# Prompt attention with value products of two key blocks issued together

## The chip, the cores and the metric

The kernel runs on one core of a Trainium2 chip. The metric is device time in microseconds (us) of one execution; shorter is better. The core has a matrix engine (PE; PEld is its weight load), a vector engine (DVE), an activation engine (ACT), a general engine (POOL), which also issues the gathers by index, and SP, whose queue issues the other DMAs. Each engine runs its own instructions in a fixed order and waits for the others by semaphores.

## What is computed

One inference step of a one-layer decoder for a prompt of 1024 tokens and a sample group of 8 x 4 tokens, in float32. The stage that matters here is the attention of the prompt, for each block of 128 queries, with 8 heads in 2 groups:

```python
d_c = pos_q[:, None] - c_end[None, :]
s = jnp.einsum('bghtd,bgnd->bghtn', q, ck) * scale - slope * d_c
p_c = masked_probs(s, d_c >= 0)
o_c = jnp.einsum('bghtn,bgnd->bghtd', p_c, cv)            # compressed keys
...
o_s = jnp.einsum('bghtn,bgtnd->bghtd', p_s, vs)           # selected blocks
...
o_w = jnp.einsum('bghtl,bgld->bghtd', p_w, vw)            # window of 512
o = gate[0] * o_c + gate[1] * o_s + gate[2] * o_w
```

With 16 blocks of 64 keys in the prompt and the best 16 selected, the selected branch of the prompt is plain causal attention. The sample group does the same over 2048 cached tokens, of which it gathers the selected pages, and both groups also attend to 256 memory tokens.

## The kernel before, in words

The work is written as a Python program whose instructions a scheduler lays out once, ahead of time, into one order for each engine; it interleaves independent parts. Attention lies between the input projections and the output projection, at about 655 to 1067 us of the span. Three things run there side by side: the prompt's attention (`nsa_prompt`), the prompt's memory attention (`mem_unit`), and the sample group (`sample`).

The prompt's attention goes over 8 query blocks j, 2 head groups g and two branches b (causal and window); each (j, g, b) is a unit. A unit has three steps:

- **heads** (B): for each of 4 heads one or two tiles of scores S. Two matmuls (L837, L840) and masks (L839) make the scores, DVE takes the maximum (L845), ACT the exponential (L846) into a tile P. L840 needs QB, half of which POOL writes for each (j, g) in `prep` (L788).
- **fin**: the factors, and P times them (L878).
- **drain** (D): the unit's items are its key blocks of 128 and, in one branch, 63 compressed keys (cvp). For an item k, `tstep(k)` transposes P of the four heads on PE into one bank T (L891, two banks) and ACT copies T to PT in the buffer memory (L893, three buffers); `pvstep(k)` does two matmuls of 64 output columns each (L905), one for each half of the output partitions, that add V times PT to O (one bank). At the last item of both branches DVE multiplies O by the gates (L908) and SP stores it.

Drain steps wait in a queue of up to 14 and are woven between the heads of later units; in program order it is T0, T1, O0, T2, O1, T3, O2 and so on. There are 148 items in all.

The sample group works in two halves Q of four sequences, each in groups c = 4, 0, 1, 2, 3 of 512 keys. A group transposes its keys (L1495), multiplies them with the queries (L1502), and multiplies the probabilities with the values (L1527). Its rows lie in xs, seven buffers; for c = 0 to 3 POOL gathers them by index (L1336), four gathers in a group, and each waits until an earlier group's L1527 has freed its buffer. POOL runs in order, so a QB that stands behind gathers comes after them, and it waits for the landings of those ahead of it. New keys of the sample group are added by an extra product with VN (L1531), out of the probabilities P8 transposed (L1517).

Of the kernel before, what the change touches and what calls it, by code (L numbers as in the profile page):

```python
# [8 lines left out]
F32 = mybir.dt.float32  # L9
# [5 lines left out]
ALU = mybir.AluOpType  # L15
# [5 lines left out]
NP = 1024  # L21
# [80 lines left out]
class Build:  # L102
# [372 lines left out]
    def mem_unit(self, pool, psp, j):  # L475

        nc = self.nc
# [39 lines left out]
        PTs = []  # L517

        def tstep(k):
            def f():  # L520
                T = psp.tile([128, 512], F32, name="T", tag="T", bufs=2)
                for h in range(4):
                    o = h % 2 * 256 + k * 128
                    nc.tensor.transpose(T[:, h * 128:(h + 1) * 128], st["P"][h // 2][:, o:o + 128], self.ident)
                PT = pool.tile([128, 512], F32, name="PT", tag="PT", bufs=3)
                nc.scalar.activation(PT, T, AF.Copy)
                PTs.append(PT)
            return f
# [269 lines left out]
    def nsa_unit(self, pool, psp, j, g, b, ctx, prep, has_c):  # L798


        nc, mkb = self.nc, self.mkb
# [7 lines left out]
        for si, (a0, a1) in enumerate([(0, n0), (n0, nk)] if n0 < nk else [(0, nk)]):  # L809
            w = (a1 - a0) * 128  # L810
# [69 lines left out]
        items = []  # L880
# [3 lines left out]
        PTs = {}  # L884

        def tstep(k):
            def f():
                si, o, w, v = items[k]
                T = psp.tile([128, 512], F32, name="T", tag="T", bufs=2)
                for i in range(4):  # L890
                    nc.tensor.transpose(T[:w, i * 128:(i + 1) * 128], Ps[i, si][:, o:o + w], self.ident)  # L891
                PT = pool.tile([128, 512], F32, name="PT", tag="PT", bufs=3)
                nc.scalar.activation(PT[:w], T[:w], AF.Copy)  # L893
                PTs[k] = PT
            return f

        def pvstep(k):
            def f():
                _, _, w, v = items[k]
                if ctx["n"] == 0:  # L900
                    ctx["O"] = psp.tile([128, 512], F32, name="O", tag="O", bufs=1)
                O, n, total = ctx["O"], ctx["n"], ctx["total"]
                pv = PTs[k].rearrange("k (a c q) -> k c a q", a=2, c=2)
                for c in range(2):
                    nc.tensor.matmul(O[c * 64:(c + 1) * 64, :256], v, pv[:w, c], start=n == 0, stop=n == total - 1)  # L905
                ctx["n"] += 1
                if ctx["n"] == total:
                    nc.vector.tensor_tensor(ctx["gb"], O[:, :256], ctx["gb"], op=ALU.mult)  # L908
                    for a in range(2):
                        nc.sync.dma_start(self.s_mix[2 * g + a][:, j * 128:(j + 1) * 128], ctx["gb"][:, a * 128:(a + 1) * 128])  # L910
            return f

        def D():
            seq = [tstep(0)]
# [406 lines left out]
    def sample(self, pool, psp):  # L1321


        nc, A = self.nc, self.A
# [47 lines left out]
        for hd in range(8):  # L1372
            g, h = hd // 4, hd % 4
# [28 lines left out]
        BR = [32 * i for i in range(4)]  # L1402
# [2 lines left out]
        for b in range(8):  # L1405
            nc.sync.dma_start(run(A["new_win_s"][b, 0:508]), run(A["cache_win_kv"][b, 4:512]))

        VN = pool.tile([8, 2, 4, 128], F32, name="VN")
        nc.gpsimd.memset(VN, 0.0)
        for Q in range(2):  # L1410
            for i in range(2):
                nc.sync.dma_start(VN[i * 4:(i + 1) * 4, i], self.s_kv[1 + i][NP + Q * 16:NP + Q * 16 + 16, 128:256].rearrange("(b t) c -> t b c", t=4))

            ps = psp.tile([128, 512], F32, name="sS", tag="sS", bufs=2)
            for bb in range(4):
# [1 line left out]
            for bb in range(4):  # L1417
                b = Q * 4 + bb
# [55 lines left out]
            O = newO()  # L1474
# [6 lines left out]
            for c in (4, 0, 1, 2, 3):  # L1481
                xs = []
                for bb in range(4):
                    b = Q * 4 + bb
                    if c == 4:
                        x = load(A["cache_win_kv"][b].rearrange("(n l) f -> n l f", l=4))
                    else:
                        x = load(cslc, idx=idx4[:, c, b:b + 1])
                    xs.append(x)

                KT_ = []
                for a in range(4):
                    pt = pst()
                    for bb in range(4):
                        nc.tensor.transpose(pt[:, bb * 128:(bb + 1) * 128], xs[bb][:, a, 0:128], ident)  # L1495
                    KT_.append(pool.tile([128, 512], F32, name="KTs", tag="KTs", bufs=4))
                    evac(KT_[a], pt)
                S = psp.tile([128, 512], F32, name="sS", tag="sS", bufs=2)
                nc.tensor.matmul(S, sta[:, c], mov[:, int(c == 4)], start=True, stop=False, skip_group_check=True)
                for a in range(4):  # L1500
                    for bb in range(4):
                        nc.tensor.matmul(S[BR[bb]:BR[bb] + 32, a * 128:(a + 1) * 128], Qb[:, Q * 4 + bb], KT_[a][:, bb * 128:(bb + 1) * 128],  # L1502
                                         start=False, stop=True, skip_group_check=True)
                n_ = nm[:, c:c + 1]
                nc.vector.tensor_reduce(n_, S, axis=AX.X, op=ALU.max, negate=True)
                nw = {4: 1, 0: 0}.get(c)
                if nw is not None:
                    tt(n_, n_, nm[:, 5 + nw:6 + nw], op=ALU.min)
                    nc.scalar.activation(P8[:, nw * 4:nw * 4 + 4], SC[:, 128 + nw * 4:132 + nw * 4], AF.Exp, bias=n_, accum_out=s8[:, nw:nw + 1])
                P = pool.tile([128, 512], F32, name="sP", tag="sP", bufs=1)  # L1510
                nc.scalar.activation(P, S, AF.Exp, bias=n_, accum_out=sm[:, c:c + 1])
                if nw is not None:
                    tt(sm[:, c:c + 1], sm[:, c:c + 1], s8[:, nw:nw + 1], op=ALU.add)
                    pn = pst()
                    if nw:
                        nc.vector.memset(P8[:, 0:4], 0.0)
                    nc.tensor.transpose(pn[:8, 0:128], P8, ident)  # L1517
                    nc.vector.tensor_copy(PN, pn[:8, 0:128])
                pt = pst()
                for a in range(4):  # L1520
                    nc.tensor.transpose(pt[:, a * 128:(a + 1) * 128], P[:, a * 128:(a + 1) * 128], ident)
                PT = pool.tile([128, 512], F32, name="sPT", tag="sPT", bufs=2)
                evac(PT, pt)
                O = newO()
                for a in range(4):
                    for bb in range(4):
                        nc.tensor.matmul(O[BR[bb]:BR[bb] + 32, 0:128], PT[:, a * 128 + BR[bb]:a * 128 + BR[bb] + 32], xs[bb][:, a, 128:256],  # L1527
                                         start=a == 0, stop=a == 3 and nw is None)
                if nw is not None:
                    for bb in range(4):  # L1530
                        nc.tensor.matmul(O[BR[bb]:BR[bb] + 32, 0:128], PN[:, BR[bb]:BR[bb] + 32], VN[:, nw, bb], start=False, stop=True)  # L1531
                take(c, O)

            mn = pool.tile([128, 4], F32, name="mn", tag="mn", bufs=2)
# [306 lines left out]
```

## Time and profile before

| what | value |
|---|---|
| median of 3 runs | 2003.86 us (2001.06 to 2009.85) |
| profiled execution, device time | 2001.53 us |
| its span | 1999.8 us |
| mean granted clock of PE | 0.973 of full speed |
| PE busy | 1898.9 us, 95% of the span |
| DVE, ACT, POOL busy | 1154.1, 756.6, 434.3 us |
| attention, 655 to 1067 us of the span | 412 us: PE busy 386.84, DVE 306.05, ACT 282.69, POOL 62.40 |

A matmul's row in the trace runs from its start to a modelled end, and matmuls overlap, so what a group of matmuls costs is read from its start to the start of the next group, not from its length. Each L905 matmul leaves two records; an item's two matmuls stand as x4. "issue" is time in which an engine waited for nothing that the profile shows.

### The profile page before, as it was taken

The numbers are of one execution on the slowest core, as the hardware profiler recorded it, in microseconds if no ns is written. First come the engines' busy times: TensorE is split into PE (matmuls) and PEld (weight loads), VectorE is DVE, ScalarE is ACT, GpSimd is POOL, SyncE is SP. The second block draws the span as 40 slices with busy tenths as digits, with TensorE's granted clock in tenths as the row PEclk, the third lists the DMA queues.
The fourth block names the chain that finished last, engine by engine and source line by source line (L and its number), as shares of the span: only waits on it lengthen the run. The fifth ranks groups of instructions, "written<-read, shape, count | busy, mean of one in ns | idle before, by whom it ended". The sixth has DMA issues, their size and how long they took to land.

```text
span 1999.8 us, 33859 instructions
## 1 busy us (share of the span) xinstructions
PE 1898.9 (95%) x13280; PEld 1727.9 (86%) x13280; DVE 1154.1 (58%) x2759; ACT 756.6 (38%) x1696; POOL 434.3 (22%) x282
## 2 busy tenths in 40 slices
PE   8988999999996898999999999899999999999997
PEld 7987889999995666666657998799999999999997
DVE  6378897425535876786773216655455555544536
ACT  6301224226645576767673315122222111222222
POOL 2044331441102321022000213422121111121200
PEclk9989999999998799999999999899999999999999
DMA  7443333664336643333323322111111111111102
GB/s 267 149 132 92 101 86 96 189 184 168 114 117 133 196 138 105 125 99 103 105 86 114 87 76 88 32 53 53 43 43 53 43 43 43 43 43 53 43 1 87
DMA packets 197689, 191.31 MB, mean 96 GB/s; under 512 B 32925, under 2 KB 177046, under 8 KB 196314
## 3 DMA queue, kind: packets, MB, share of 16 engines
q1 hardware_dynamic: 190730, 153.86, 25.9%
q0 software_dynamic: 6800, 35.30, 5.3%
q8 instruction: 104, 1.70, 0.4%
q14 instruction: 55, 0.45, 0.1%
HBM read 155.34 MB, written 38.55 MB: 97 GB/s over the span
## 4 chain that ended last, share of the span: by engine, by line
PE 82%; DVE 7%; DMA 4%; issue 3%; ACT 2%; SPq 1%; POOL 1%; DVEq 0%; ACTq 0%; POOLq 0%
PE fps L122 12%; PE fps L124 12%; PE fps L123 12%; PE pso L122 4%; PE pso L124 4%; PE pso L123 4%; PE O L905 4%; PE T L891 4%; PE ops L122 2%; PE ops L124 2%; PE ops L123 2%; PE S L840 2%; PE S L837 2%; PE cps L630 1%; PE cps L122 1%
## 5 line engine op out<-in xcount | busy, mean ns | idle before, releaser
L1768 DVE TENSOR_TENSOR acc<-fps,acc 128x352 f32<-128x352 f32 (+3 forms) x360 | 185.3, 523 | 156.7 <-PE fps L124 156.7
L123 PE MATMUL fps<-h2lo,hi 128*128 128x352 f32 x768 | 248.1, 323 | 2.0 <-DVE h2lo L1712 2.0
L122 PE MATMUL fps<-h2hi,hi 128*128 128x352 f32 x768 | 247.7, 323 | 1.9 <-ACT h2hi L1711 1.9
L122 PE MATMUL fps<-yh,f2hi 128*128 128x352 f32 (+3 forms) x768 | 243.6, 326 | 6.0 <-DVE rm L1760 6.0
L123 PE MATMUL fps<-yl,f2hi 128*128 128x352 f32 (+3 forms) x768 | 247.1, 324 | 1.7 <-DVE yl L1745 1.7
L124 PE MATMUL fps<-h2hi,lo 128*128 128x352 f32 x768 | 248.7, 324 | 0.0
L124 PE MATMUL fps<-yh,f2lo 128*128 128x352 f32 (+3 forms) x768 | 246.6, 324 | 0.0
L1743 DVE TENSOR_TENSOR rl<-rl 128x352 f32<-128x352 f32 x96 | 132.0, 1376 | 145.3 <-ACT rl L1742 145.3
L118 POOL TENSOR_TENSOR lo<-raw,hi 128x1024 fp32r<-128x1024 f32 (+1 forms) x43 | 97.0, 2256 | 369.9 <-ACT hi L112 367.0
L118 POOL TENSOR_TENSOR f2lo<-raw,f2hi 128x1024 fp32r<-128x1024 f32 x32 | 79.6, 2487 | 363.1 <-ACT f2hi L112 354.9
L124 PE MATMUL pso<-hhi,wlo 128*128 128x352 f32 x480 | 157.3, 328 | 0.0
L123 PE MATMUL pso<-hlo,whi 128*128 128x352 f32 x480 | 157.2, 328 | 0.0
L122 PE MATMUL pso<-hhi,whi 128*128 128x352 f32 x480 | 157.2, 327 | 0.0
L122 PEld LDWEIGHTS fps<-yh,f2hi 128*128 128x128 f32 x768 | 144.7, 190 | 7.8 <-DVE rm L1760 6.3
L846 ACT ACTIVATE P<-S,nst 128x384 f32<-128x384 f32 (+4 forms) x264 | 127.3, 489 | 57.7 <-DVE nst L845 45.1
L123 PEld LDWEIGHTS fps<-yl,f2hi 128*128 128x128 f32 x768 | 145.5, 190 | 3.5 <-DVE yl L1745 2.0
L123 PEld LDWEIGHTS fps<-h2lo,hi 128*128 128x128 f32 x768 | 145.0, 189 | 2.3 <-DVE h2lo L1712 2.3
L122 PEld LDWEIGHTS fps<-h2hi,hi 128*128 128x128 f32 x768 | 144.9, 189 | 2.2 <-ACT h2hi L1711 2.2
L124 PEld LDWEIGHTS fps<-yh,f2lo 128*128 128x128 f32 x768 | 145.5, 190 | 1.4
L124 PEld LDWEIGHTS fps<-h2hi,lo 128*128 128x128 f32 x768 | 145.7, 190 | 0.0
L845 DVE TENSOR_REDUCE nst<-S 128x1 f32<-128x384 f32 (+4 forms) x264 | 109.8, 434 | 59.5 <-PE S L840 42.3
L112 ACT ACTIVATE f2hi<-raw 128x1024 fp32r<-128x1024 f32 x32 | 33.8, 1059 | 284.3 <-PE fps L123 269.1
(594 smaller groups left out, 4519.0 us busy)
## 6 DMA issues: line engine op xcount, KB each, us to landing
raw<-w_ff SPq DMA_DIRECT2D x64, 512.0 KB
wraw<-w_in SPq DMA_DIRECT2D x28, 512.0 KB
xs<-cache_mem_kv SPq DMA_DIRECT2D x16, 512.0 KB
s_gb<-st SPq DMA_DIRECT2D x36, 176.0 KB
x<-x_prompt SPq DMA_DIRECT2D x8, 512.0 KB
wraw<-w_mem_kv SPq DMA_DIRECT2D x8, 512.0 KB
qd<-s_q SPq DMA_DIRECT2D x32, 128.0 KB
ngb<-s_gb SPq DMA_DIRECT2D x64, 64.0 KB
```

Source lines behind the costliest of these rows:

```text
L118: eng.tensor_tensor(lo, src, hi.bitcast(F32), op=ALU.subtract)
L122: mm(ps, ahi, bhi, start=start, stop=False)
L123: mm(ps, ahi, blo, start=False, stop=False)
L124: mm(ps, alo, bhi, start=False, stop=stop)
L837: nc.tensor.matmul(S[:, :w], ctx["QA"][:, qs], KA[:, k0:k0 + w], start=True, stop=False)
L840: nc.tensor.matmul(S[:, :w], ctx["QB"][:, qs], KB[:, k0:k0 + w], start=False, stop=True)
L845: nc.vector.tensor_reduce(t[:, 0, pi, i:i + 1], S[:, o:o + pw], axis=AX.X, op=ALU.max, negate=True)
L846: nc.scalar.activation(P[:, o:o + pw], S[:, o:o + pw], AF.Exp, bias=t[:, 0, pi, i:i + 1], accum_out=t[:, 1, pi, i:i + 1])
L891: nc.tensor.transpose(T[:w, i * 128:(i + 1) * 128], Ps[i, si][:, o:o + w], self.ident)
L905: nc.tensor.matmul(O[c * 64:(c + 1) * 64, :256], v, pv[:w, c], start=n == 0, stop=n == total - 1)
L1743: tt(r, r, r, op=ALU.mult)
L1768: tt(acc[:, m, o:o + n], ps[:, :n], acc[:, m, o:o + n], op=ALU.add)
```

## The change

`pvstep` of an even item does nothing, unless it is the last; `pvstep` of an odd item k does the products of k and then of k - 1. So two items' products come one behind the other, after the transposes of the item that follows them. PT has four buffers in place of three, and for the room VN is halved: the two new-key parts lie in one tile, and P8's other half is zeroed each time (two more small memsets on DVE, one large one less on POOL).

```diff
-                PT = pool.tile([128, 512], F32, name="PT", tag="PT", bufs=3)
+                PT = pool.tile([128, 512], F32, name="PT", tag="PT", bufs=4)
...
         def pvstep(k):
             def f():
-                _, _, w, v = items[k]
-                if ctx["n"] == 0:
-                    ctx["O"] = psp.tile([128, 512], F32, name="O", tag="O", bufs=1)
-                O, n, total = ctx["O"], ctx["n"], ctx["total"]
-                pv = PTs[k].rearrange("k (a c q) -> k c a q", a=2, c=2)
-                for c in range(2):
-                    nc.tensor.matmul(O[c * 64:(c + 1) * 64, :256], v, pv[:w, c], start=n == 0, stop=n == total - 1)
-                ctx["n"] += 1
...
+
+                if k % 2 or k == len(items) - 1:
+                    pv1(k)
+                if k % 2:
+                    pv1(k - 1)
             return f
+
+        def pv1(k):
+            _, _, w, v = items[k]
+            if ctx["n"] == 0:
+                ctx["O"] = psp.tile([128, 512], F32, name="O", tag="O", bufs=1)
+            O, n, total = ctx["O"], ctx["n"], ctx["total"]
+            pv = PTs[k].rearrange("k (a c q) -> k c a q", a=2, c=2)
+            for c in range(2):
+                nc.tensor.matmul(O[c * 64:(c + 1) * 64, :256], v, pv[:w, c], start=n == 0, stop=n == total - 1)
+            ctx["n"] += 1
...
-        VN = pool.tile([8, 2, 4, 128], F32, name="VN")
-        nc.gpsimd.memset(VN, 0.0)
+        VN = pool.tile([8, 4, 128], F32, name="VN")
...
-                    if nw:
-                        nc.vector.memset(P8[:, 0:4], 0.0)
+                    nc.vector.memset(P8[:, 4 - nw * 4:8 - nw * 4], 0.0)
...
-                        nc.tensor.matmul(O[BR[bb]:BR[bb] + 32, 0:128], PN[:, BR[bb]:BR[bb] + 32], VN[:, nw, bb], start=False, stop=True)
+                        nc.tensor.matmul(O[BR[bb]:BR[bb] + 32, 0:128], PN[:, BR[bb]:BR[bb] + 32], VN[:, bb], start=False, stop=True)
```

The scheduler lays the whole of attention out anew. In the changed kernel L905 is L913, L1495 is L1501 and L1336 is L1343; L788, L837, L840 and L891 keep their numbers.

PE at the end of the last unit's drain, before (T are transposed blocks, O<-PT,V the products; the copy of T_n is PT_(n+5)):

```order
L905 MATMUL O_12789<-PT_12853,V1_6841 64x256 x2
L891 MATMUL T_12864<-ident_103,P_12630 128x128
L891 MATMUL T_12864<-ident_103,P_12663 128x128
L891 MATMUL T_12864<-ident_103,P_12698 128x128
L891 MATMUL T_12864<-ident_103,P_12731 128x128
L905 MATMUL O_12789<-PT_12860,V1_6841 64x256 x2
```

and after:

```order
L891 MATMUL T_12856<-ident_103,P_12631 128x128
L891 MATMUL T_12856<-ident_103,P_12662 128x128
L891 MATMUL T_12856<-ident_103,P_12697 128x128
L891 MATMUL T_12856<-ident_103,P_12732 128x128
L891 MATMUL T_12863<-ident_103,P_12631 128x128
L891 MATMUL T_12863<-ident_103,P_12662 128x128
L891 MATMUL T_12863<-ident_103,P_12697 128x128
L891 MATMUL T_12863<-ident_103,P_12732 128x128
L913 MATMUL O_12797<-PT_12861,V1_6841 64x256 x2
L913 MATMUL O_12797<-PT_12854,V1_6841 64x256 x2
```

Four transposes and one item's products in turn have become eight transposes and two items' products, the newer item's first.

POOL in the second half of the sample group, around the QBs of query block 6 (QB_11514 and 11741 before, QB_11515 and 11742 after; xs are gathered pages), before:

```order
L1336 DMA xs_8309<-cache_slc_kv,idx4_7260 128x1024 [waits PE_49]
L1336 DMA xs_8311<-cache_slc_kv,idx4_7260 128x1024 [waits DMASW7_49,PE_49]
L788 TENSOR_SCALAR QB_11514<-augq_6812,augj_6814 64x512 [waits DMASW3_49,DMASW2_49,DMASW4_49,DMASW1_49,DMASW5_49,DMASW0_49,DMASW6_49,DVE_49,PE_49]
L788 TENSOR_SCALAR QB_11741<-augq_6812,augj_6814 64x512 [waits DVE_49,PE_49]
L1336 DMA xs_8313<-cache_slc_kv,idx4_7260 128x1024 [waits PE_49,Pool_49]
L1336 DMA xs_8390<-cache_slc_kv,idx4_7260 128x1024 [waits PE_49]
L1336 DMA xs_8392<-cache_slc_kv,idx4_7260 128x1024 [waits PE_49]
L1336 DMA xs_8394<-cache_slc_kv,idx4_7260 128x1024 [waits PE_49]
```

and after:

```order
L1343 DMA xs_8310<-cache_slc_kv,idx4_7260 128x1024 [waits PE_49]
L1343 DMA xs_8312<-cache_slc_kv,idx4_7260 128x1024 [waits DMASW7_49,PE_49]
L1343 DMA xs_8314<-cache_slc_kv,idx4_7260 128x1024 [waits DMASW0_49,PE_49]
L1343 DMA xs_8391<-cache_slc_kv,idx4_7260 128x1024 [waits DMASW1_49,PE_49]
L1343 DMA xs_8393<-cache_slc_kv,idx4_7260 128x1024 [waits DMASW2_49,PE_49]
L1343 DMA xs_8395<-cache_slc_kv,idx4_7260 128x1024 [waits DMASW3_49,PE_49]
L788 TENSOR_SCALAR QB_11515<-augq_6812,augj_6814 64x512 [waits DMASW4_49,DMASW2_49,DMASW5_49,DMASW1_49,DMASW6_49,DMASW0_49,DMASW7_49,DVE_49,PE_49]
L788 TENSOR_SCALAR QB_11742<-augq_6812,augj_6814 64x512 [waits DVE_49,PE_49]
```

Both QBs now stand behind four more gathers, those that the sample product of group c = 1 sets free.

PE at the first use of that QB, before:

```order
L891 MATMUL T_11532<-ident_103,P_11264 128x128
L1521 MATMUL sS_8281<-ident_103,sP_8279 128x128 [waits Activation_49]
L1521 MATMUL sS_8281<-ident_103,sP_8279 128x128 x3
L837 MATMUL S_11558<-KA00_6816,QA_11513 128x448 [waits Activation_49]
L839 LDWEIGHTS idb_6810
L839 MATMUL S_11558<-mkb_6808,idb_6810 128x64
L840 MATMUL S_11558<-KB00_6820,QB_11514 128x448 [waits DVE_49,Pool_49]
```

and after:

```order
L1501 MATMUL sS_8337<-ident_103,xs_8308 128x128 [waits Activation_49]
L1501 MATMUL sS_8337<-ident_103,xs_8310 128x128
L1501 MATMUL sS_8337<-ident_103,xs_8312 128x128
L1501 MATMUL sS_8337<-ident_103,xs_8314 128x128
L840 MATMUL S_11559<-KB00_6820,QB_11515 128x448 [waits Pool_49]
L840 MATMUL S_11568<-KB00_6820,QB_11515 128x512
L837 MATMUL S_11575<-KA00_6816,QA_11514 128x448 [waits Activation_49]
```

The first use stood ahead of the product of group c = 1; it stands now behind that product and all 16 key transposes of group c = 2.

## Rows read from the trace of the kernel before

**Rows 1.** Page, part 1: busy time, share of the span, instructions.

```profile
PE 1898.9 (95%) x13280; PEld 1727.9 (86%) x13280; DVE 1154.1 (58%) x2759; ACT 756.6 (38%) x1696; POOL 434.3 (22%) x282
```

**Rows 2.** Busy time by stretch of attention: engines' us (instructions), PE clock, DMA share, GB/s.

```profile
740.00:780.00 40.00, 33.63 (x296) 23.72 (x296) 25.53 (x79) 22.86 (x68) 7.96 (x7) 0.91 0.44 131
...
860.00:900.00 40.00, 39.72 (x362) 27.07 (x360) 33.10 (x112) 27.73 (x87) 6.76 (x6) 1.00 0.40 118
...
1040.00:1067.00 27.00, 23.05 (x154) 12.81 (x154) 17.25 (x55) 18.55 (x48) 0.00 (x0) 1.00 0.21 64
```

**Rows 3.** Waits of PE in 655 to 1067 us: total us, times, longest.

```profile
PE S L840 <- POOL QB L788: 6.6, 2, 5.9
PE O L905 <- ACT PT L893: 6.1, 9, 1.6
```

**Rows 4.** Timeline at the end of the drain: start, us, engine, line, operation, xrecords.

```profile
1061.24 0.65 PE L905 MATMUL O<-PT,V 128*64 128x256 f32 x4
...
1061.82 0.66 PE L891 MATMUL T<-ident,P 128*128 128x128 f32 x4
...
1062.41 0.65 PE L905 MATMUL O<-PT,V 128*64 128x256 f32 x4
1062.58 0.60 ACT L893 ACTIVATE PT<-T 128x512 f32<-128x512 f32 x1 [0.57 <-PE T L891]
```

**Rows 5.** Timeline: transposes before scores, and two items' products in a row.

```profile
863.53 0.66 PE L891 MATMUL T<-ident,P 128*128 128x128 f32 x4
...
863.95 0.42 PE L837 MATMUL S<-KA,QA 128*128 128x384 f32 x1
...
867.24 1.08 PE L905 MATMUL O<-PT,V 128*64 128x256 f32 x8
...
868.25 0.44 PE L837 MATMUL S<-KA,QA 128*128 128x384 f32 x1
```

**Rows 6.** Timeline: sample product, scores before scores, scores before products, memory scores.

```profile
740.14 1.08 PE L1527 MATMUL sS<-xs,sPT 128*32 128x128 f32 x32
...
741.76 0.42 PE L840 MATMUL S<-KB,QB 128*128 128x384 f32 x1
...
742.02 0.34 PE L837 MATMUL S<-KA,QA 128*128 128x384 f32 x1
...
742.24 0.42 PE L840 MATMUL S<-KB,QB 128*128 128x384 f32 x1
...
742.58 0.65 PE L905 MATMUL O<-PT,V 128*64 128x256 f32 x4
...
745.36 0.28 PE L123 MATMUL S<-mklo,QA 128*128 128x256 f32 x1
...
745.48 0.28 PE L124 MATMUL S<-mkhi,QB 128*128 128x256 f32 x1
```

**Rows 7.** Timeline: one matmul of an item by itself (two records).

```profile
895.71 0.64 PE L905 MATMUL O<-PT,cvp 63*64 63x256 f32 x2
896.28 0.39 PE L1499 MATMUL sS<-smov,ssta 36*128 36x512 bf16 x1
```

**Rows 8.** POOL's timeline: gathers and QBs, with the idle time ahead and its releaser.

```profile
745.29 0.94 POOL L1336 DMA_INDIRECT xs<-cache_slc_kv,idx  x1 [0.30 <-PE S L840]
753.08 3.22 POOL L788 TENSOR_SCALAR QB<-augq,augj 64x512 fp32r<-64x512 bf16 x2 [6.85 <-issue]
...
922.89 3.22 POOL L788 TENSOR_SCALAR QB<-augq,augj 64x512 fp32r<-64x512 bf16 x2 [8.96 <-PE S L840]
931.05 1.18 POOL L1336 DMA_INDIRECT xs<-cache_slc_kv,idx  x1 [4.95 <-PE sS L1527]
...
935.06 0.95 POOL L1336 DMA_INDIRECT xs<-cache_slc_kv,idx  x1 [0.30 <-issue]
```

**Rows 9.** Gathers' line: DMA from issue to landing.

```profile
DMA to landing us min/median/max: 5.6/6.4/7.4
```

**Rows 10.** Stretch of 2 us behind the stall, columns as in Rows 2.

```profile
758.00:760.00 2.00, 2.00 (x10) 0.96 (x9) 1.48 (x6) 1.09 (x5) 0.00 (x0) 0.55 0.00 0
```

More of the change, by code (lines that the diff above doesn't have):

```diff
@@ L891, in f @@
                     nc.tensor.transpose(T[:w, i * 128:(i + 1) * 128], Ps[i, si][:, o:o + w], self.ident)
-                PT = pool.tile([128, 512], F32, name="PT", tag="PT", bufs=3)
+                PT = pool.tile([128, 512], F32, name="PT", tag="PT", bufs=4)
                 nc.scalar.activation(PT[:w], T[:w], AF.Copy)
@@ L898, in f @@
             def f():
-                _, _, w, v = items[k]
-                if ctx["n"] == 0:
-                    ctx["O"] = psp.tile([128, 512], F32, name="O", tag="O", bufs=1)
-                O, n, total = ctx["O"], ctx["n"], ctx["total"]
-                pv = PTs[k].rearrange("k (a c q) -> k c a q", a=2, c=2)
-                for c in range(2):
-                    nc.tensor.matmul(O[c * 64:(c + 1) * 64, :256], v, pv[:w, c], start=n == 0, stop=n == total - 1)
-                ctx["n"] += 1
[L907 to L910, printed above, removed]
-            return f
+                if k % 2 or k == len(items) - 1:
+                    pv1(k)
+                if k % 2:
+                    pv1(k - 1)
+            return f
+        def pv1(k):
[7 more added lines that the diff above has]
+            ctx["n"] += 1
+            if ctx["n"] == total:
+                nc.vector.tensor_tensor(ctx["gb"], O[:, :256], ctx["gb"], op=ALU.mult)
+                for a in range(2):
+                    nc.sync.dma_start(self.s_mix[2 * g + a][:, j * 128:(j + 1) * 128], ctx["gb"][:, a * 128:(a + 1) * 128])
         def D():
@@ L1406, in sample @@
             nc.sync.dma_start(run(A["new_win_s"][b, 0:508]), run(A["cache_win_kv"][b, 4:512]))
-        VN = pool.tile([8, 2, 4, 128], F32, name="VN")
-        nc.gpsimd.memset(VN, 0.0)
+        VN = pool.tile([8, 4, 128], F32, name="VN")
         for Q in range(2):
             for i in range(2):
-                nc.sync.dma_start(VN[i * 4:(i + 1) * 4, i], self.s_kv[1 + i][NP + Q * 16:NP + Q * 16 + 16, 128:256].rearrange("(b t) c -> t b c", t=4))
+                nc.sync.dma_start(VN[i * 4:(i + 1) * 4], self.s_kv[1 + i][NP + Q * 16:NP + Q * 16 + 16, 128:256].rearrange("(b t) c -> t b c", t=4))
             ps = psp.tile([128, 512], F32, name="sS", tag="sS", bufs=2)
```

## The prediction

> **What bounds the kernel now.** I read the page's busy times first: PE is busy 95% of the span and no other engine over 58% [rows 1]. Then the stretches of attention, since nothing outside it changes its work: in the stretch from 860 us PE is busy 39.72 of 40 us, while DVE has 33.10 and ACT 27.73; the stretch from 740 us has a hole (33.63 of 40, clock 0.91), and the last one, from 1040 us, another (23.05 of 27) with ACT at 18.55 [rows 2]. So PE time is worth its full length in most of attention, and little at its end. PE's waits name two of the holes: 6.6 us for QB, of which 5.9 in one wait, and 6.1 us in nine waits for a copy PT ahead of products [rows 3]. The reader is to see that PE's order has about 26 us of holes in 412 (412 less the 386.84 of the table), so a gain has to come out of PE's own instructions, and a new wait of a few us undoes much of it.
>
> **What a switch costs.** One item's products take 0.58 us to the start of the next transposes, and four transposes 0.59 us to the start of the next products [rows 4]. Two items in a row take 1.01 us to the scores behind them [rows 5], so the second item costs 0.43 and each run of products pays 0.15 us when PE leaves it. Four transposes ahead of scores take 0.42 [rows 5], so entering products from transposes costs 0.17. Scores of 384 columns take 0.26 us ahead of scores and 0.34 ahead of products [rows 6]: entering from scores costs 0.08.
>
> **The change, part by part.**
>
> *Fewer runs.* PE's order, counted: the 148 items stand in 141 runs of products before and in 83 after, 58 fewer. Leaving: 58 x 0.15 = 8.7 us. Entering from transposes (50 to 29): 21 x 0.17 = 3.6. From scores (58 to 37): 21 x 0.08 = 1.7. From the sample group's work (33 to 17), which no row prices: 16 between 0.08 and 0.17, 1.3 to 2.7; I take the middle, 2.0. Together 16.0 us less on PE, nearly all where PE is the bound.
>
> *Split items.* One of an item's two matmuls by itself takes 0.57 us [rows 7], as long as both together [rows 4]; torn apart, an item costs 0.43 more. The scheduler tears 3 items before and 5 after: 2 x 0.43 = 0.9 us lost.
>
> *Compressed keys in a run.* An item of 63 keys stands beside one of 128 in 3 places before and in 14 after. No row separates that switch from a wait for the copy. Bounds: 0, as inside a run, and 0.15, as on leaving one; 11 x 0 to 0.15 = 0 to 1.7 us. I take 0.8, the middle. The Trainium skill, page "TensorEngine Tiling (Array Packing)", section Key Properties, says that a change of the tiling mode, not of the tile alone, drains TensorE; whether 63 rows count as another mode it doesn't say. By it the loss is the upper end and the sum 0.9 us worse; no row here decides.
>
> *The wait for the newest copy.* After the transposes of k + 1 the products of k come first, whose copy is the newest but one, with one block of transposes between. Where only drain is left (five runs in the order), the two blocks of transposes take 0.42 + 0.59 = 1.01 us from the start of the first, while its copy ends 1062.58 + 0.60 - 1061.82 = 1.36 us after it [rows 4]: PE waits 0.35 us, a pair takes 1.01 + 0.35 + 1.01 = 2.37 instead of 2 x 1.17 = 2.34, and the gain there is gone. Elsewhere heads and sample work lie between: by the durations above the distance from a block's first transpose to its products is about 3.3 us in the middle of the list in both orders, and under 1.36 us in 3 items before and 10 after, 2.7 us short more than before. Today's waits for copies are 6.1 us though only three items are so near [rows 3], because ACT has other work ahead of the copy. I charge 3 us more; bounds 0 (the waits of today, halved in number, balance it) and 8 (they double, and the ten come on top).
>
> *The stall for QB at query block 3 stays.* POOL's QB there waits for gathers that a sample product sets free: the product starts at 740.14 [rows 6], the last of its four gathers is issued at 745.29, QB starts at 753.08, and two QBs take 3.22, so the first is there at 754.69, 14.6 us after the product [rows 8]. Nothing in that chain gets faster. PE has 2 runs fewer between (0.5 us) and one score head of 384 columns and its mask (0.56) moved behind it, so it comes 1.1 us earlier and waits 1.1 us longer than the 5.9 [rows 3]. 1.1 us lost.
>
> *A new stall for QB at query block 6.* Before, its QBs started at 922.89, released by PE, ahead of the gathers of 931.05 to 935.06 [rows 8]. In the new order four more gathers stand ahead of them, those that the product of group c = 1 frees, and POOL's QB waits for their landing. On PE there lie between that product's start and the first L840 that reads QB: 16 sample products (1.0 us), 16 key transposes and 16 transposes of P (32 x 0.105 = 3.4, a quarter of the 0.42 each), 4 items (4 x 0.43 = 1.7) in 3 runs (3 x 0.27 = 0.8 of switches), 12 memory score matmuls of 0.12 us, start to start (1.4) [rows 6], and five score matmuls with their masks at 0.26 (1.3): 9.6 us. The chain of the stall above took 14.6 us; with the shortest landing, 5.6 us [rows 9], it is 745.29 - 740.14 = 5.2 plus 5.6 plus 1.6 = 12.4. PE therefore waits 2.8 to 5.0 us; I take 5.0, the difference to the chain that the trace shows whole. The clock answers to such a wait: in the stretch from 758 us, behind the stall of 5.9 us, the granted clock is 0.55 [rows 10], so it was at the lower of its two levels (1.2 GHz) for 1.8 of the 2 us. If so ever since the stall's end at 754.7, that is 5.1 us of work that take 2.5 at 2.4 GHz. The new stall is a little shorter: I charge 2.0; bounds 0 and 2.5.
>
> *The rest.* A fourth PT takes a wait away from ACT only; no row shows ACT late for want of a buffer, so nothing. POOL loses a memset and DVE gains two small ones: neither engine is the bound [rows 2], nothing. The reads of VN come later than one half's did, which can delay a load of the second half of the sample group on SP; its reader is far behind, nothing.
>
> **Sum.** 16.0 - 0.9 - 0.8 - 3.0 - 1.1 - 5.0 - 2.0 = 3.2 us faster. Against the profiled execution, 2001.5 us of device time (span 1999.8), that is 1998.3. The median of the three runs lies 2.3 us above that execution, and the comparison will be with runs like them, so I set the forecast at 2003.9 - 3.2 = 2000.7 us. About 0.5%, 10 us, is what a measurement of this kernel can tell from no change.
>
> **The rivals.**
>
> *A, the new stall doesn't open.* If the gathers land faster at that place, or PE reaches the L840 late because it waited for keys and copies that would have cost it time anyway, 5.0 + 2.0 come back: gain 10.2, time 1993.7 us. For it: PE needs one of the same gathers for its key transposes ahead of the L840, so part of the wait is shared; landings vary from 5.6 to 7.4 us [rows 9]. Against: even the fastest chain is 2.8 us longer than PE's work.
>
> *B, slower: the newest copy rules.* ACT's copies come behind exponentials, and in each of the 58 merged places PE waits 0.35 us or more, as in the pure drain: 58 x 0.35 = 20 us in place of the 3. Then 3.2 + 3 - 20 = -14, time 2018 us. It turns the change into a loss from (3.2 + 3) / 0.35 = 18 places on. For it: the product wants the newer copy first. Against: the middle distance of 3.3 us is over twice the 1.36 us that a copy needs, and ACT has a quarter to a third of its time free where PE is bound [rows 2].
>
> *C, nothing comes through.* Other engines take PE's place as soon as it gets faster: DVE, at 33.10 of 40 us in the dense stretch [rows 2], has the least room. Gain 16.0 - 0.9 - 0.8 all gone into waits for scores, with the old stalls longer by as much: 2003.9 us. Against: DVE would be at 86% of the time if all 16 us came off attention.
>
> **How the numbers follow.** My forecast (stall and copies about as charged) 0.60 at 2000.7; A 0.22 at 1993.7; B 0.06 at 2018; C 0.12 at 2003.9. With every bound of my own case at its best end (0.7 more from entering, 0.8 from compressed keys, 3 from copies, 4.2 from the new stall) it would be 1992, at its worst (0.7, 0.9, 5 and 0.5) 2008. Faster by over 0.5% means below 1993.8: A's better half and the best end of my own case, 0.18. Slower by over 0.5%, above 2013.9: B, 0.06. Within 0.5%: 0.76. The range takes in all but B and the outer ends of A: 1991 to 2009.
>
> **What would show each step.** In the changed kernel's trace: two items' products in a row as x8 of about 1.01 us to the next start, some 58 times; PE's busy time in attention down by some 14 us while its waits are up by 8 to 10; one wait of PE at L840 for POOL QB of 6 to 8 us near 750 us and a second one of 3 to 6 us, not there before, near 890 to 900 us, with the clock at half behind both; waits of products for PT between 6 and 12 us, and 0.35 us in each pair at the end of the drain. The end of attention should come some 3 us earlier and all behind it be unchanged. I am wrong if the second stall isn't there (A), if products wait for PT by over 15 us (B), or if DVE is what PE's scores wait for (C).

## The result, and the profile after

The changed kernel takes 2016.95 us (median of 8 runs) where the kernel before takes 2002.45 (8 runs beside it): a ratio of 1.0072, 95% interval 1.0055 to 1.0089. It is 14.5 us slower; the forecast was 3.2 us faster, and the range ended at 2009.

Its profiled execution has a span of 2016.6 us. Nothing outside attention moved: attention starts 0.8 us earlier than before, and what follows attention takes 0.8 us longer, out of some 927. Attention grew. This is the page's row of busy times, against [rows 1]:

```profile
PE 1897.7 (94%) x13280; PEld 1740.2 (86%) x13280; DVE 1155.7 (57%) x2761; ACT 754.2 (37%) x1696; POOL 432.3 (21%) x281
```

PE is as busy as before although 58 runs of products fewer leave less to do; so part of its work ran slower. The stretches of attention (columns as in [rows 2]) show where, and the second fence has all of attention in the kernel before:

```profile
641.00:1089.00 448.00, 398.19 (x3309) 280.52 (x3309) 315.68 (x1025) 288.02 (x885) 63.38 (x50) 0.92 0.38 113
...
740.00:780.00 40.00, 30.46 (x277) 22.07 (x269) 23.99 (x74) 20.09 (x62) 8.08 (x7) 0.91 0.44 130
860.00:900.00 40.00, 38.67 (x337) 28.14 (x336) 31.72 (x103) 24.23 (x76) 8.10 (x8) 0.89 0.35 104
920.00:960.00 40.00, 34.04 (x316) 22.20 (x315) 22.12 (x66) 22.19 (x68) 7.03 (x7) 0.91 0.27 74
```

```profile
642.00:1073.00 431.00, 401.54 (x3309) 270.75 (x3308) 313.26 (x1023) 290.38 (x885) 63.97 (x50) 0.94 0.39 117
```

The same 3309 matmul records take 448 us instead of 431, with 50 us instead of 29 in which PE has nothing, and at a mean granted clock of 0.92 instead of 0.94. PE's waits in 655 to 1085 us (total us, times, longest), against [rows 3]:

```profile
PE S L840 <- POOL QB L788: 16.5, 3, 6.5
PE sS L1501 <- DMA xs<-cache_slc_kv,idx: 7.9, 3, 3.1
PE S L837 <- ACT P L846: 7.3, 3, 3.7
PE T L891 <- ACT PT L893: 4.9, 7, 1.4
PE O L913 <- ACT PT L893: 3.6, 10, 0.7
PE T L891 <- DVE P L878: 2.7, 2, 1.5
```

In the kernel before the first two were 6.6 [rows 3] and 1.8 us:

```profile
PE sS L1495 <- DMA xs<-cache_slc_kv,idx: 1.8, 4, 0.6
```

The waits for the copy PT have mostly moved from the products (6.1 us) to the transposes, which fill two T in a row and have only two.

This is the new stall at query block 6, from the timelines of PE and POOL:

```profile
927.23 1.08 PE L1532 MATMUL sS<-xs,sPT 128*32 128x128 f32 x32
...
932.32 0.95 POOL L1343 DMA_INDIRECT xs<-cache_slc_kv,idx  x1 [0.30 <-issue]
...
936.52 1.04 PE L1501 MATMUL sS<-ident,xs 128*128 128x128 f32 x8
...
941.66 3.22 POOL L788 TENSOR_SCALAR QB<-augq,augj 64x512 fp32r<-64x512 bf16 x2 [8.39 <-DVE P L515]
943.28 1.17 PE L840 MATMUL S<-KB,QB 128*128 128x448 f32 x2 [5.72 <-POOL QB L788]
```

The sample product at 927.23 frees the pages, the last of four gathers goes out at 932.32, QB starts 9.3 us later, and PE stands for 5.72 us. The gathers of this place (two of the four have a landing in the trace) took

```profile
DMA to landing us min/median/max: 7.9/8.4/8.9
```

so the last landed at 932.3 + 8.9 = 941.2 us, and QB starts 0.4 us later. The row names a DVE instruction that ended at about the same time; in a second profile of this kernel the last landing again lies 0.4 us ahead of QB and that DVE instruction ends 0.8 us before the landing, so the landing is what QB waits for. Behind the stall, and behind the wait for gathered pages that ends at 967.7, stretches of 2 us (the last three columns: granted clock, DMA share, GB/s):

```profile
943.00:945.00 2.00, 1.72 (x5) 1.19 (x5) 0.74 (x2) 0.41 (x2) 1.79 (x2) 0.50 0.00 0
945.00:947.00 2.00, 2.00 (x9) 0.77 (x8) 0.87 (x3) 0.00 (x0) 0.00 (x0) 0.50 0.04 8
947.00:949.00 2.00, 2.00 (x13) 0.91 (x11) 0.00 (x0) 0.00 (x0) 0.00 (x0) 0.98 0.00 0
...
967.00:969.00 2.00, 1.29 (x5) 1.09 (x6) 0.77 (x2) 0.57 (x2) 0.00 (x0) 0.64 0.91 301
969.00:971.00 2.00, 2.00 (x11) 1.60 (x10) 1.15 (x3) 1.58 (x7) 0.00 (x0) 0.51 0.21 56
```

After either wait PE works at 1.2 GHz (0.50) for 3 to 4 us before the grant returns to 2.4.

### The profile page after: what moved, and what is told of

It is laid out like the page before. It is cut to its first block, busy times and chain, and to the rows that moved or that the text cites. A ratio compares the mean times of both kernels' runs of the same rounds, so it can differ in the third digit from the quotient of the medians.

```text
span 2016.6 us, 33796 instructions
## 1 busy us (share of the span) xinstructions
PE 1897.7 (94%) x13280; PEld 1740.2 (86%) x13280; DVE 1155.7 (57%) x2761; ACT 754.2 (37%) x1696; POOL 432.3 (21%) x281
## 4 chain that ended last, share of the span: by engine, by line
PE 48%; DVE 2%; issue 1%; ACT 1%; DMA 1%; POOL 0%; DVEq 0%; SPq 0%; POOLq 0%; ACTq 0%
PE fps L122 12%; PE fps L124 12%; PE fps L123 12%; PE ops L122 2%; PE ops L124 2%; PE ops L123 2%; PE O L913 1%; PE T L891 1%; PE S L840 1%; DVE acc L1729 0%; PE S L837 0%; DMA mxr<-s_mix 0%; DMA xs<-cache_slc_kv,idx 0%; PE fps L1790 0%; DVE P L878 0%
```

## Attention taken apart

The same account was made for every kernel that was run. Length: from the matmul of L672 at attention's start to the first `ops` matmul that waited for the last copy. Waits: time in that stretch with no matmul record on PE. Lost at half clock: busy time at 1.2 GHz, from the granted clock of 1-us stretches, halved, since the same work would take half as long at 2.4 (an estimate). Rest: what is left, PE's work at full clock. Ratios are to the kernel before in the same comparison, with their 95% intervals.

| kernel (runs of products) | ratio | length | waits | lost at half clock | rest |
|---|---|---|---|---|---|
| before (141) | | 431.3 | 29.5 | 21.2 | 380.6 |
| unpaired_again, the same | 1.0001 (0.9975 to 1.0027) | 429.0 | 30.6 | 17.4 | 381.0 |
| changed (83) | 1.0072 (1.0055 to 1.0089) | 448.1 | 49.9 | 29.8 | 368.5 |
| paired_again, the same | 1.0096 (1.0054 to 1.0139) | 447.1 | 51.4 | 27.3 | 368.4 |
| no_pair (141) | 1.0002 (0.9985 to 1.0019) | 429.6 | 29.4 | 21.3 | 378.9 |
| pair_3pt (83) | 1.0083 (1.0064 to 1.0101) | 442.9 | 47.4 | 26.1 | 369.3 |
| old_first (121) | 1.0047 (1.0028 to 1.0066) | 434.7 | 37.9 | 19.9 | 376.8 |
| unpaired_13p (144) | 1.0053 (1.0036 to 1.0070) | 442.2 | 34.1 | 29.2 | 378.9 |
| pair_13p (80) | 0.9997 (0.9984 to 1.0011) | 430.0 | 36.2 | 28.6 | 365.2 |
| unpaired_b10 (142) | 1.0040 (1.0021 to 1.0059) | 431.2 | 33.6 | 16.4 | 381.2 |
| before_qb_dve (143) | 1.0010 (0.9994 to 1.0026) | 430.5 | 29.0 | 18.4 | 383.0 |
| after_qb_dve (81) | 0.9948 (0.9931 to 0.9965) | 413.7 | 29.7 | 14.1 | 369.9 |
| pair_qb6_dve (83) | 0.9986 (0.9974 to 0.9998) | 424.6 | 38.6 | 17.8 | 368.2 |
| pair_qb13_dve (84) | 0.9930 (0.9908 to 0.9951) | 412.9 | 24.1 | 17.4 | 371.4 |
| pair_13p_qb_dve (82) | 0.9938 (0.9917 to 0.9960) | 419.7 | 30.2 | 21.6 | 367.9 |
| pair_qb_act (84) | 0.9908 (0.9877 to 0.9940) | 414.0 | 27.4 | 15.1 | 371.6 |

Each row is one profiled execution; its length stands within some 7 us of what the ratio says. The last column hardly moves with the execution and falls into two groups: 379 to 383 us without pairing, 365 to 372 with it; old_first, whose pairs are mostly torn apart again, has 377. From before to changed: rest 12.1 less, waits 20.4 more, half clock 8.6 more, 16.9 in all.

## The experiments

Theory G: the pairing saves its switches, and the chain of gathers, the QBs queued behind them and the clock behind the stalls eat more than that. Theory C: the products wait for the newest copy. Theory L: any new order of the scheduler's moves the time by as much, pairing or not.

**Attention alone.** In both kernels `name="xs", tag="xs", bufs=7` became `bufs=8`: the sample group's space no longer fits beside attention's, and it is finished ahead.

> The kernel before with an eighth buffer for the sample group's pages: the space on the right side no longer fits beside attention's, so the whole sample group is finished ahead of attention, and attention runs alone (no gather, key transpose or sample product between its heads and drains, all QBs on POOL with no gather ahead). The computation is the same. It is the base for the next run; the time itself goes well above the kernel before's, by the sample group's own chain, since nothing fills its waits (an estimate: 50 to 250 us more). All theories: same base.

> The same eighth buffer in the changed kernel: attention alone, products in 80 runs where the run before has 144. Theory G (pairing does save its switches; the gathers' chain and the half clock behind its stalls eat them): with no gathers beside it attention gets 64 x 0.15 = 9.6 us shorter for leaving products and some 4 to 6 for entering, less the waits for newer copies: 8 to 16 us faster than before_alone. Theory C (newest copy: products wait for ACT, and that is the loss): no gain or a loss, 0 to 15 us slower than before_alone. Theory L (layout: any new order of the scheduler's moves the time by this much): between -10 and +15, no sign forecast.

Measured: 2094.24 and 2082.68 us, 11.6 us apart by the medians of 4 runs each; by the ratios to the kernel before (1.0481, 1.0444 to 1.0518, and 1.0439, 1.0405 to 1.0472) 8.4. The two intervals overlap, but each run of the unpaired kernel is slower than every run of the paired one. Attention by itself in the two, unpaired and paired (columns as in [rows 2]):

```profile
822.00:1162.00 340.00, 317.08 (x2101) 204.51 (x2101) 252.66 (x836) 257.82 (x804) 28.26 (x15) 0.97 0.18 51
```

```profile
818.00:1147.00 329.00, 302.30 (x2104) 208.32 (x2103) 250.18 (x834) 255.00 (x804) 25.20 (x15) 0.98 0.19 53
```

The same matmuls keep PE busy 14.8 us less; 3 of that are time at half clock, and the rest in the sense of the table falls from 304.8 to 292.8. With no gathers beside it pairing is a gain of the size forecast: G holds, C doesn't (waits for copies rose from 12.6 to 15.4 us only).

**QB off POOL.** `nc.gpsimd.tensor_scalar(QB[64:128], ...)` became `nc.vector.tensor_scalar(...)` in both kernels, and in the changed one, as a second remedy, an activation on ACT:

```
-            nc.gpsimd.tensor_scalar(QB[64:128], self.augq[64:128, ...], self.augj[64:128, j:j + 1], None, op0=ALU.mult)
+            nc.scalar.activation(QB[64:128], self.augq[64:128, ...], AF.Copy, scale=self.augj[64:128, j:j + 1])
```

> The kernel before with QB's lower half written by DVE instead of POOL: it can't stand behind gathers any more. The scheduler lays attention out anew; 140-odd runs of products stay. Theory G: of the 6.6 us that PE waits for QB nearly all goes, and about 2 of half clock behind; DVE pays 16 times some 0.7 us beside PE: 3 to 8 us faster than the kernel before. Theories C and L: within 5 us of it, either way.

> The changed kernel with QB's lower half written by DVE instead of POOL; 81 runs of products. Theory G: PE's 16.5 us of waits for QB and some 6 us of half clock behind three of them go, part of it (a third) into waits for the gathered pages themselves, which PE now reaches earlier: 10 to 22 us faster than the changed kernel, so at or below the kernel before, 1995 to 2007 us, and 0 to 10 us below before_qb_dve. Theory C: the waits for copies stay, 2010 us or more. Theory L: no sign forecast.

> The changed kernel with all QBs' lower halves written by ACT instead of POOL (84 runs of products): another engine for the same remedy. ACT also writes QA and the copies PT, DVE has its old load. Theory G: POOL's queue was the cost, so ACT does as well as DVE did: 1980 to 1992 us. If DVE's time was what bounds it, 2 to 6 us faster than after_qb_dve (1985.6); if ACT's copies are late behind it, slower than that.

Measured: 1998.63, 1985.61 and 1982.33 us where the kernel before had 1998.27, 1998.27 and 1999.03 beside them. The pairing is worth 13.0 us here (1998.63 to 1985.61), and the changed kernel gains 25 us by its ratio from moving one operation, a little over the 10 to 22 expected. (Like nearly every edit here, it also makes the scheduler lay attention out anew, so the 25 us are QB's move and a new layout together.) PE's waits in after_qb_dve, 655 to 1067 us:

```profile
PE T L891 <- ACT PT L893: 4.7, 6, 2.0
...
PE O L913 <- ACT PT L893: 3.4, 8, 0.9
...
PE sS L1501 <- DMA xs<-cache_slc_kv,idx: 2.2, 2, 1.6
```

The waits for copies are nearly those of the changed kernel (8.1 us, there 8.5), and yet the kernel is below the one before: that is what refutes C. Those for QB are gone, and those for gathered pages fell from 7.9 to 2.2 us: they did not grow, against what was expected. ACT does it as well as DVE or better; the two were not timed side by side, and the intervals touch. The 3.3 us between the medians also lie in the range of that run's rival (DVE's time bounds it), which stays open. The kernel before gains nothing, though 3 to 8 us were expected: its waits for QB went, but others (a copy QA of 2.1, an sPT of 1.9) stand in their place. pair_qb_act is 0.9908 of the kernel before: faster than both kernels of the change.

**The other parts of the change, and the order within a pair.** no_pair is the kernel before with four PT and the new VN and P8; pair_3pt the changed kernel with three PT and the old VN and P8; old_first swaps the pair:

```
-                if k % 2 or k == len(items) - 1:
-                    pv1(k)
                 if k % 2:
                     pv1(k - 1)
+                if k % 2 or k == len(items) - 1:
+                    pv1(k)
```

> The kernel before with all of the change but the pairing: four buffers for PT, one half of VN, the two clearings of P8 on DVE. 141 runs of products, POOL's order of gathers and QBs as in the kernel before. Theory G and theory C: within 4 us of the kernel before. Theory L (any new order moves the time): up to 15 us off it, either way.

> The pairing alone: three buffers for PT and the VN of before; 83 runs of products, 10 items torn, POOL's order as in the changed kernel but for one gather. The prediction gave the fourth buffer nothing. If that holds: within 4 us of the changed kernel, as slow as it. If the fourth buffer carries weight (with three, a copy of the next pair waits until a pair's products are done): 5 us or more slower than it.

> The changed kernel with the older block's products ahead of the newer one's. The scheduler then pulls most pairs apart again: 121 runs of products instead of 83. POOL's order keeps the QBs of query block 6 behind six gathers as in the kernel before, not behind ten. Theory C (the products wait for the newest copy): faster than the changed kernel by the copies' waits, and near the kernel before less 20 runs, 3 to 4 us below it. Theory G: the same sign by another reason, the new stall of 5.7 us and the half clock behind it gone and the gathers' waits shorter: 1996 to 2005 us where the kernel before has some 2000. The waits of products for copies in the trace tell the two apart: C wants them 5 us or more below the changed kernel's, G the QB waits 6 us or more below its 16.5.

Measured: 1996.95, 2013.22 and 2007.66 us, beside 1997.34, 1997.62 and 1997.34 of the kernel before. The rest of the change costs nothing, and the fourth buffer gives nothing, as the prediction had it. (The expectations' counts of gathers ahead of the QBs of query block 6, six and ten, are rows of the order; in gathers they are 8 before, 12 in the changed kernel. And pair_3pt has 5 torn items like the changed kernel, not 10.) In old_first products wait for copies 2.4 us instead of 3.6. C's mark, 5 us less, could not be met, since the changed kernel has only 3.6 us of such waits in all; what speaks against C is that they are so few, and that with fewer of them old_first is still 9.4 us slower than the kernel before. Of G's marks the waits for QB fell by 7.6 us as wanted, the time missed the range: the gathers' waits stayed. PE's waits in 655 to 1080 us:

```profile
PE S L840 <- POOL QB L788: 8.9, 2, 7.3
PE sS L1501 <- DMA xs<-cache_slc_kv,idx: 8.7, 3, 4.1
```

**Other layouts.** `self.pbufs = 14` became 13, with and without pairing; `self.backlog = 14` became 10 without.

> The changed kernel with 13 instead of 14 buffers for the probabilities P: 80 runs of products, so the pairing is whole, but POOL's QBs of query block 6 stand behind six gathers again as in the kernel before. Theory G: the wait of 5.7 us at that place and 2 to 3 us of half clock behind it go; those near 676 and 748 us and the gathers' stay: 5 to 12 us faster than the changed kernel, if one buffer fewer costs nothing. Theory C: as slow as the changed kernel.

> The kernel before with 13 instead of 14 buffers for P: 144 runs of products, no pairing, POOL's order as in the kernel before. It tells how much of pair_13p's time is due to the 13 buffers. Theory G: within 4 us of the kernel before, so that pair_13p, 1 us below that one, is the pairing's own saving less longer waits at the gathers. Rival: the ring of 13 by itself is faster by 5 us or more.

> The kernel before with a drain backlog of 10 instead of 14 steps: no pairing (142 runs of products), but POOL's QBs of query block 6 stand behind ten gathers in a row as in the changed kernel. Theory G: a wait of PE for QB of 4 to 6 us near 890 to 940 us with half clock behind it, 5 to 9 us slower than the kernel before. Theory C: no products behind the newest copy, so no more than 3 us from the kernel before. Theory L: no sign forecast.

Measured: 1996.34, 2008.77 and 2005.07 us, beside 1997.34, 1997.62 and 1997.34. Pairing gives 12.4 us once more (2008.77 to 1996.34; 11 by the ratios, since the two were not timed side by side), now with all QBs on POOL. pair_13p is 15 us below the changed kernel by the ratios, more than the 5 to 12 expected. But the rival to unpaired_13p came true in reverse: 13 buffers alone cost the kernel before 11 us. PE's waits in the two, unpaired and paired:

```profile
PE S L840 <- POOL QB L788: 8.2, 2, 7.6
PE sS L1495 <- DMA xs<-cache_slc_kv,idx: 7.6, 4, 2.2
```

```profile
PE S L840 <- POOL QB L788: 9.3, 2, 8.9
PE sS L1501 <- DMA xs<-cache_slc_kv,idx: 7.5, 4, 2.8
```

The gathers' waits are as long without pairing as with it: they belong to the layout. So half of L's claim holds: without any pairing, two small edits moved the time by 8 and 11 us. unpaired_b10 has 10 gathers ahead of the QBs of query block 6 and no wait for QB there. But it doesn't test G: the two gathers more are early ones, and the four that the product of group c = 1 frees (at 925.27 us) come behind the QBs (918.95), as in the kernel before. That its 8 us lie in G's range of 5 to 9 is luck. Where they come from stays open; its profiled execution (span 1998.0), the fastest of its ten, has an attention as long as the kernel before's. pair_13p_qb_dve, the changed kernel with 13 buffers and all QBs on DVE, took 1986.33 us where 1981 to 1990 were expected: with QB off POOL the 13 buffers show no loss.

**One stall at a time.** Only some QBs on DVE: `(nc.vector if j == 6 else nc.gpsimd).tensor_scalar(QB[64:128], ...)`, and the same with `j in (1, 3)`.

> The changed kernel with the two QBs of query block 6 alone written by DVE, all others by POOL; 83 runs of products as in the changed kernel, and POOL's order the same but for these two. Theory G: PE's wait of 5.7 us at 937 goes, and with it the 5 to 6 us of work at half clock behind it, 2.5 us; up to a third comes back as a wait for the gathered pages: 4 to 9 us faster than the changed kernel. Rival (the wait isn't the cost: PE would wait for the gathers there anyway): 0 to 2 us.

> The changed kernel with the QBs of query blocks 1 and 3 on DVE, that of block 6 and all others on POOL; 84 runs of products; a memory of the stall that the kernel before has as well. Theory G: the waits for QB near 676 and 748 us go (4.3 or less, and 6.5) with 3 to 5 us of half clock behind them, the one at 938 stays: 6 to 14 us faster than the changed kernel, 2003 to 2011 us where the kernel before has some 2000. Rival (only the stall that is new counts, the old one is paid in another coin): no more than 3 us.

Measured: 1994.78 us, 0.9986 of the kernel before, so by the ratios 17 us below the changed kernel; and 1986.72, 0.9930. Both gained far more than expected. In pair_qb6_dve the stretch that had the new stall is full (the first fence, columns as in [rows 2]), and two kinds of waits shrink (the second, PE's waits in 655 to 1062 us):

```profile
920.00:960.00 40.00, 39.94 (x375) 28.08 (x363) 30.13 (x92) 29.44 (x90) 4.74 (x5) 1.00 0.49 143
```

```profile
PE S L840 <- POOL QB L788: 7.9, 2, 7.6
PE sS L1501 <- DMA xs<-cache_slc_kv,idx: 5.8, 2, 3.7
```

Not only the wait of 5.7 us went, also the gathers' wait of 2.5 behind it, those for scores near 1041 and 1046 us, and half clock with them: 11.3 us of waits and 12.0 of half clock by the table, 12.8 and 9.5 against the second profile of the changed kernel. The wait of 4.3 us near 676 went too, though nothing was moved there; of it below. In pair_qb13_dve the stall of query block 6 should have stayed and did not, though its QBs stand behind 12 gathers on POOL as in the changed kernel (timelines of POOL and PE):

```profile
898.94 1.02 POOL L1343 DMA_INDIRECT xs<-cache_slc_kv,idx  x1 [0.30 <-PE S L840]
907.44 1.56 POOL L788 TENSOR_SCALAR QB<-augq,augj 64x512 fp32r<-64x512 bf16 x1 [7.49 <-PE S L840]
912.21 1.57 POOL L788 TENSOR_SCALAR QB<-augq,augj 64x512 fp32r<-64x512 bf16 x1 [3.21 <-PE S L124]
...
912.60 0.45 PE L840 MATMUL S<-KB,QB 128*128 128x448 f32 x1
```

The sample group's second half starts its first four gathers at 852 us here, at 884 in the changed kernel's second profile; the QB has been there for 3.6 us when PE asks for it at 912.60. This corrects G: the number of gathers ahead doesn't decide, but how long PE works between the sample product that frees their pages and the first head that needs QB. Here that product starts at 893.81, 18.8 us before PE asks for QB, and QB is there after 15.2. In the changed kernel the distance is 10.3 us (927.23 to 937.56), and QB is there after 16.0. The new layout set that distance; that the early stalls were what shifted it is not shown.

**Both kernels again.**

> The changed kernel itself, profiled a second time. Open: which of its new waits belong to its order and which to one execution. Theory G wants the waits for QB near 748 and 938 us and the gathers' near 778 and 965 us again, each within 2 us of the first profile's (6.5, 5.7, 3.1, 2.5). The 4.3 us at 676 may be one execution's: it comes from the gathers' landing behind the start of the sample group, and the same place has 0.3 to 1.6 us in three neighbours of this order.

> The kernel before itself, profiled a second time: its wait of 5.9 us for QB at 749 again within 2 us, the share of attention in neither waits nor half clock (380.6 us from the first profile) within 2 us. If that share moves by more than 4 us between two executions, the 12 us between unpaired and paired kernels is not as firm as it looks.

Measured: 2018.76 and 2000.35 us. Waits of PE in the second profile of the changed kernel, 655 to 1085 us, and in that of the kernel before:

```profile
PE S L840 <- POOL QB L788: 13.9, 2, 7.5
PE sS L1501 <- DMA xs<-cache_slc_kv,idx: 9.1, 3, 3.4
PE S L837 <- ACT P L846: 8.2, 6, 3.7
PE T L891 <- ACT PT L893: 4.0, 6, 1.3
PE O L913 <- ACT PT L893: 3.6, 10, 0.7
```

```profile
PE S L840 <- POOL QB L788: 8.6, 2, 6.2
...
PE O L905 <- ACT PT L893: 5.1, 10, 1.1
PE sS L1495 <- DMA xs<-cache_slc_kv,idx: 2.5, 3, 1.2
```

The waits near 748 (7.5), 779 (3.4), 942 (6.4) and 967 us (3.0) are there again; that of 4.3 us at 676 is not, and the kernel before has one of 2.4 there this time: it belongs to the execution. "Rest" moved by 0.4 us at most between two executions of one kernel.

## The prediction, step by step

*Fewer runs, torn items, compressed keys:* right in kind and nearly in size. 14.3 us were forecast net, 12.1 and 12.6 came. The sign named for it, PE's busy time in attention down by some 14 us, failed: it fell by 3.4 (401.54 to 398.19), because more of the work ran at half clock. Part of the difference in size is the compressed keys: the middle of 0 to 0.15 us was taken, and the timeline of the changed kernel shows the upper end. From an item of 63 keys to one of 128 it takes 0.58 us, not the 0.43 of two alike:

```profile
1080.74 0.65 PE L913 MATMUL O<-PT,cvp 63*64 63x256 f32 x4 [0.68 <-ACT PT L893]
1081.32 0.65 PE L913 MATMUL O<-PT,V 128*64 128x256 f32 x4
1081.90 0.43 PE L122 MATMUL ops<-mxh,w0hi 128*128 128x352 f32 x1
```

All 14 such places have 0.57 to 0.59, so 11 x 0.15 = 1.7 us were lost and the net is 13.4; the last 1 us or so stays open. The Trainium skill, page "TensorEngine Tiling (Array Packing)", section Key Properties, says that a change of the tiling mode drains TensorE. The trace agrees with the reading that 63 rows against 128 are such a change, at 0.15 us each; it doesn't show the drain itself.

*The newest copy:* right in size, wrong in place. 3.0 us were charged; waits of products and transposes for copies together went from 6.1 to 8.5 us in the first pair of profiles, from 5.1 to 7.6 in the second. But the products, which were to wait 6 to 12 us, wait less than before (3.6); the transposes, which the prediction didn't name, wait 4.9. In the pure drain a pair takes 2.36 us, forecast 2.37, with a wait of 0.25, forecast 0.35:

```profile
1069.98 1.09 PE L891 MATMUL T<-ident,P 128*128 128x128 f32 x8
1071.32 1.08 PE L913 MATMUL O<-PT,V 128*64 128x256 f32 x8 [0.25 <-ACT PT L893]
1072.34 1.09 PE L891 MATMUL T<-ident,P 128*128 128x128 f32 x8
```

Rival B gave 2018 us and so the right time, but by 20 us of such waits; its reason fell. So did A's (the new stall opened) and C's (scores waited only 0.4 us for DVE).

*The stall at query block 3, 1.1 us longer:* right, 0.65 in the first pair of profiles, 1.3 in the second.

*The new stall at query block 6, 5.0 us:* right in kind, 5.72 and 6.39, somewhat over the upper bound. From the product's start PE worked 10.3 us, forecast 9.6, and QB took 16.0, forecast 14.6: the last gather needed 8.9 us to land, more than any in the trace of the kernel before (7.4) [rows 9]. The place, given as 890 to 900 us, was wrong: PE came to the stall at 937.6.

*The half clock behind it, 2.0 us:* right for that one place (3.8 us of busy time at 1.2 GHz, 1.9 lost), wrong as the whole of the term. Over attention the loss grew by 8.6 us, and by 9.9 in the second pair.

*What the sum did not hold:* waits for the gathered pages themselves, up from 1.8 to 7.9 us (2.5 to 9.1 in the second pair), near 699, 779 and 967 us. The prediction followed the gathers to the QBs behind them; their first reader, PE's key transposes, which wait on the same landing, it named only in rival A, as a reason for a shorter stall, and charged nothing for. It didn't hold the wait for QB of 4.3 us at 676 either, which belongs to the first execution (the second has none there).

*The failed step* is the sum's wait and clock terms. They were 3.0 + 1.1 + 5.0 = 9.1 us of new waits and 2.0 of half clock; 20.4 and 8.6 came (20.8 and 9.9 in the second pair). The sum took today's holes as fixed outside the places that it walked through, while the scheduler had laid out all of attention anew, and it charged the clock at one place only. (A slip without weight: 412 less 386.84 is 25 us of holes, not 26.)

The bounds, 1992 to 2008 us, were bounds of the terms listed, with nothing for the scatter of layouts, which the runs without pairing put at 8 to 11 us.

That the new order, and not the pairing as such, made the loss is shown: in four unpaired and paired couples (alone, QB on DVE, 13 buffers, and this kernel) the rest fell by 12 to 14 us each time, and in the first three the time fell by 11.6 to 13.0 (8 to 12 by the ratios). The times alone would not show it, since layouts scatter by as much; the rest does. Which decision of the scheduler's turned the sample group against the heads was not traced.

## What to carry over

Where a scheduler lays out a stretch anew for an edit, cost the edit's own work from rows, as here, but give the range the scatter of layouts as well: one or two neutral edits that are timed show it. Follow every long transfer to all of its readers, those queued behind it on its own engine too, and ask how much work the bound engine has between what starts it and what needs it; a faster engine comes to the wait sooner. An operation that only shares a queue with such transfers is worth trying on another engine: in the changed kernel that turned a loss of 14.5 us into a gain of 13 (DVE) and 17 (ACT) by the medians, a new layout included; in the kernel before it gained nothing.

## What the runs showed beyond that

A wait of PE costs more than its length. In the changed kernel each of the waits from 2.3 to 6.5 us inside attention was followed by PE at 1.2 GHz, for 3.3 us or more, which lost 1.5 to 3 us (4.5 behind 854 us, where a second wait follows). Through the runs the two shares rise together only roughly: pair_qb6_dve has more waits than unpaired_13p (38.6 and 34.1 us) and loses less by the clock (17.8 and 29.2). Some waits of 1.5 to 2 us were followed by it too, one of 2.2 us (pair_qb_act, at 694) not; what sets that these runs don't tell.
